# A two-layer decoder trunk on one core: weight splits around the norms move from GpSimd to VectorE in a new order, and u and the gates use three 256-column products

## The chip, the cores and the metric

The kernel runs on 1 core of one Trainium2 chip. The metric is the time of one execution in microseconds (us) of device time, lower is better.

## The reference

Two decoder layers over 256 tokens with 2048 features, in float32. Cut to what matters here:

```python
# layer 0: one input projection, its columns split into q, k, v, the forget gates, and u
proj = x @ w_in                       # 2048 -> 3*1024 + 8 + 1024
fox  = forgetting_attention(q, k, v, f_logit + b_f)     # 8 heads x 128
y    = s5_scan(u, ...)                                  # 64 groups x 16 channels, complex state of 64
ssm  = glu(gelu(y) @ w_glu)
mix  = concat(fox, ssm) @ w_out
# layer 1: sliding-window attention instead, 32 q heads / 4 kv heads x 64
# every layer:
x = LN(alpha*x + mix)
x = LN(alpha*x + (silu(gate) * val) @ w_down)   # gate, val: causal 3-wide conv of x @ w_up, d_ff 5504
```

## The kernel before

**Products in two parts.** Every weight comes as float32 in chunks of 128 x 1024 (512 KB) and is split into a high part `hi`, which ScalarE casts to the matmul type (line 110), and a rest `lo = raw - hi`, which VectorE subtracts (line 115). The activations `xT` are split in the same way: `xT[:, k, 0]` is the high part and `xT[:, k, 1]` the rest, for each of 16 blocks `k` of 128 features. A product is hi·hi + hi·rest + lo·hi; the last of the four is left out. There are two forms:

- `bmm` (line 412) has the weights stationary. It multiplies the 512 columns of `xT[:, k]` (high part and rest, 256 tokens each) by `hi`, into the two halves of a PSUM bank, and then the 256 high columns by `lo`, into the second half. `joined` (line 417) adds the halves: ScalarE copies the second half to SBUF, and VectorE adds the first.
- `amm` (line 421) has the activations stationary and streams 512 columns of weights, in three products into one bank.

**The stream.** `Stream` holds the list of all chunks in the order of use. SP loads them into 5 raw buffers. `done` frees the chunk just used, splits what there is room for (4 pairs of `hi` and `lo` at most are held) and then steps the side generators (`pump`), which record a little VectorE, ScalarE and TensorE work of the scan (`s5_gen`), the attention heads and so on between the weight chunks. So the order on every engine is the order in which the Python code runs; each engine works its queue strictly in that order, and waits where a semaphore of another engine is missing.

**The start (lines 1338 to 1385).** u is computed in 8 tiles of 128 columns, two chunks each, in two rounds of four tiles (`bmm`, 8 per chunk). After the second chunk of a tile, `joined` makes `ut`, the ScalarE queue sends `ut` to memory (line 1357), and after every second tile the GpSimd queue fetches it back in another layout (`load_u4`, line 1336). The chunk of the forget gates follows (16 `bmm`, then `joined` into `ft`, which `fox_gate` transposes at line 1232), then v (`a_run`). Beside all this VectorE prepares the scan: tables (`tab`), turned on TensorE at line 1040, and GpSimd multiplies phasors (lines 294 to 296).

**The boundaries.** There are three places where a layer norm stands between two big products (`boundary`): after the mixer of layer 0, after its FFN, and after the mixer of layer 1. The last 8 chunks before it (`tail`) and the first 8 after it (`head`) are each run twice, for token block `tb` 0 and 1, so that TensorE has work while the norm is computed. The first four chunks of the head are held in the usual pairs; the other four are split into free room of a later tensor ("places"). Lists of steps, one per chunk, say what is recorded between the products:

- `s` splits the next chunk; `s0` and `s1` interleave the split in quarters (line 127) with the statistics of block 0 or 1 (`ln_stats`);
- `n` and two digits: the norm of block tb, quarter q (`norm`, one VectorE instruction of 128x512 at line 228);
- `t`: TensorE turns that quarter (4 transposes, line 500), ScalarE scales it (line 504) and casts its high part (line 508);
- `l`: VectorE subtracts the rest of that quarter (line 213). An `amm` of the head on it needs both parts.

`PLAN_TAIL` runs beside the second pass of the tail, `PLAN_MID` between tail and head, and `PLAN_HEAD` beside the head: its first 8 entries stand behind head chunks 0 to 7 of block 0, the others behind those of block 1. `POOL_LO` sends the subtraction of the last head chunk (7) to GpSimd.

Of the kernel before, what the change touches and what calls it, by code (L numbers as in the profile page):

```python
# [21 lines left out]
P = 128  # L22
T = 256
D = 2048
KT = D // P
# [4 lines left out]
LCH = 4  # L30
# [15 lines left out]


PLAN_TAIL = "s0 n00 n01", "s n02", "s", "s", "t00", "t01 n03", "l00", "t02 l01"
PLAN_MID = "s1 l02"
PLAN_HEAD = ("s", "t03 n10 l03 n11", "", "s n12 n13 s", "", "t10", "t11 l10", "l11 t12",  # L50
             "t13 l12", "", "l13", "", "", "", "", "")
POOL_LO = {"t": (), "h": (7,)}

C_ID, C_TRI, C_CM, C_BM, C_M8, C_IF, C_N = 0, 128, 256, 384, 512, 520, 528

# [1 line left out]
class Stream:  # L57
# [31 lines left out]
    def split_next(self, steps=None, late=False):  # L89


        i = self.split
        size, dst = self.items[i][1:]
        r = self.raws.pop(i)[:, :size]
        eng = self.nc.vector
        if dst is None:
            hi = self.parts.tile([P, CH], F32R, tag="hi", name=f"hi{i}")
            lo = self.parts.tile([P, CH], F32R, tag="lo", name=f"lo{i}")
            self.held += 1
            o = hi[:, :size], lo[:, :size]  # L100
        elif dst[0] == "x":
            o = dst[1:]
            r = r.rearrange("p (a b) -> p a b", a=o[0].shape[1])
        else:
            o = [t_[:, :size] for t_ in self.places[dst[1]](dst[2])]
            self.busy.add(dst[1:3])
            if dst[3]:
                eng = self.nc.gpsimd
        hi, lo = o
        self.nc.scalar.copy(hi, r)  # L110
        self.outs[i] = o
        self.split += 1

        def rest():
            eng.tensor_tensor(lo, r, hi.bitcast(F32), op=ALU.subtract)  # L115
            self.out -= dst is None or dst[0] != "x"
            self.load()

        if late:
            return rest  # L120
        if steps is None:
            rest()
            return
        next(steps)
        m = size // 4
        for c in range(0, size, m):
            eng.tensor_tensor(lo[:, c:c + m], r[:, c:c + m], hi[:, c:c + m].bitcast(F32), op=ALU.subtract)  # L127
            next(steps, None)
            next(steps, None)
        for _ in steps:  # L130
            pass
        self.out -= 1
        self.load()
# [67 lines left out]
def trunk(ctx: ExitStack, tc: tile.TileContext, A, out):  # L201
    nc = tc.nc
    V, S, PE, G = nc.vector, nc.scalar, nc.tensor, nc.gpsimd
# [14 lines left out]
    def add(o, a, b):  # L218
        tt(o, a, b, ALU.add)
# [13 lines left out]
    def mm(o, l, r, start, stop):  # L233
        PE.matmul(o, lhsT=l, rhs=r, start=start, stop=stop)  # L234
# [84 lines left out]
    xT = mk(xtp, [P, KT, 2, T], F32R)  # L319
# [12 lines left out]

    def ext(place, c):

        return ("at", place, c - 4, c in POOL_LO[place[0]]) if c >= 4 else None

    for i0 in (0, 4):
        for h in range(2):
# [72 lines left out]
    def bmm(ps, hi, lo, k, first, last):  # L411


        mm(ps, hi, xT[:, k].rearrange("p a t -> p (a t)"), first, False)
        mm(ps[:, T:], lo, xT[:, k, 0, :], False, last)

    def joined(o, ps, view=lambda a: a):
        S.copy(o, view(ps[:, T:]))  # L418
        add(o, o, view(ps[:, :T]))

    def amm(o, hi, lo, src, k, tb, first, last):

# [64 lines left out]
    def boundary(li, tail, resid, after_tail, head):  # L487
# [3 lines left out]
        with tc.tile_pool(name="lnp", bufs=1) as lp:  # L491
# [50 lines left out]
            after_tail()  # L542
            do(PLAN_MID)
            part = []
            for c in range(8):
                part.append(st.get())
                head(part[c], 0, c)
                do(PLAN_HEAD[c])
            for c in range(8):
# [790 lines left out]
    for i0 in (0, 4):  # L1340
        ps = [bank(acc) for _ in range(4)]
        for c in range(2):
            for i in range(i0, i0 + 4):
                hi, lo = st.get()
                xs = 4 if i == 0 else 0
                for _ in range(xs):
                    st.get()
                o = ps[i - i0]
                for j in range(8):
                    bmm(o, hi[:, j * P:(j + 1) * P], lo[:, j * P:(j + 1) * P], 8 * c + j, c + j == 0, c == 1 and j == 7)  # L1350
                for _ in range(xs):
                    st.free()
                st.done()
                if c == 1:
                    ut = mk(s5w, [P, LCH, NCH], tag="ut", bufs=2)
                    joined(ut, o, lambda a: a.rearrange("p (n l) -> p l n", l=LCH))
                    S.dma_start(out=ud[P * i:P * i + P], in_=ut)
                    if i % 2 == 1:
                        load_u4(i // 2)
                    if i == 2:  # L1360
                        consts_round()
# [4 lines left out]
    ps = bank(acc)  # L1366
    hi, lo = st.get()
    for k in range(KT):
        bmm(ps, hi[:, 8 * k:8 * k + P], lo[:, 8 * k:8 * k + P], k, k == 0, k == KT - 1)
    st.done()  # L1370
    ft = mk(fp, [8, T])
    joined(ft, ps[0:8])
    gate = st.add(fox_gate(ft, fp))


# [10 lines left out]
    for h in range(H0):  # L1386
        qk = []
        for j in range(2):
            ps = bank(acc)
            b_tile(ps, 2)  # L1390
            t_ = mk(fp, [P, T], tag=f"qk{j}", bufs=2)
            if j == 0:
                c = 1.0 / math.sqrt(128.0)
# [9 lines left out]
    for cc, a, b in O0:  # L1403
# [12 lines left out]
        if b == 4:  # L1416
            for tb in range(2):
                o = stash[:, tb, cc * 512:(cc + 1) * 512]
# [10 lines left out]
    for ks in (range(0, 6), range(6, 8)):  # L1429
        for c in range(4):  # L1430
            hi, lo = part[c]
# [31 lines left out]
    last = [[bank(acc), bank(acc)] for _ in range(2)]  # L1463
# [131 lines left out]
```

## Time and profile before

| | us |
|---|---|
| median of 3 runs | 2136.7 (2136.3 to 2136.89) |
| the profiled execution | 2135.78 |
| its span | 2134.0 |
| TensorE matmul busy | 2089.1 (98%) |
| VectorE busy | 1464.5 (69%) |
| ScalarE busy | 1110.9 (52%) |
| GpSimd busy | 74.7 (3%) |

The profiled execution's own time is its span and 1.8 us around it; it lies 0.9 us under the median. Matmuls are pipelined, so their busy time is a sum of overlapping records; how fast TensorE works is read from the distance of their starts, and what it loses from the waits.

### The profile page before, as it was taken

How to read it: one execution, taken by the hardware profiler on the slowest of the kernel's cores; microseconds unless marked ns; L12 is line 12 of the kernel's file. 1: busy time of each engine (PE TensorE's matmuls, PEld its weight loads, DVE VectorE, ACT ScalarE, POOL GpSimd, SP SyncE). 2: the span in 40 equal slices, each digit the busy share in tenths (PEclk: the TensorE clock that was granted, in tenths of full speed). 3: DMA queues.
4: the chain of work that ended last, by engine and by line, in shares of the span. 5: the costliest groups of instructions: out<-in, count | busy, mean ns of one | idle time of the engine just before them, and what ended most of it. 6: DMA issues, size and time to landing. Idle time of an engine off the chain costs nothing.

```text
span 2134.0 us, 29675 instructions
## 1 busy us (share of the span) xinstructions
PE 2089.1 (98%) x11084; PEld 1759.7 (82%) x11084; DVE 1464.5 (69%) x2325; ACT 1110.9 (52%) x1766; POOL 74.7 (3%) x143
## 2 busy tenths in 40 slices
PE   8899999999999999999999999999999999999997
PEld 7688878788888888888887878778888888888886
DVE  6888866868777777744446867678777777754445
ACT  4355455566555555533336566475555555543332
POOL 3600000000000000000001000000000000000000
PEclk9999999999999999999999999999999999999999
DMA  7454455656656666566565634647666666666564
GB/s 264 151 154 135 129 193 173 202 177 213 191 188 189 190 193 189 180 192 191 183 192 165 191 119 129 197 152 229 192 190 188 189 194 190 188 188 190 185 188 158
DMA packets 111456, 388.84 MB, mean 182 GB/s; under 512 B 13072, under 2 KB 15120, under 8 KB 111056
## 3 DMA queue, kind: packets, MB, share of 16 engines
q1 hardware_dynamic: 104112, 371.37, 55.5%
q10 hardware_dynamic: 5712, 10.20, 1.9%
q0 software_dynamic: 1488, 5.38, 0.8%
q8 instruction: 87, 1.43, 0.3%
q14 instruction: 57, 0.47, 0.1%
HBM read 383.75 MB, written 3.15 MB: 181 GB/s over the span
## 4 chain that ended last, share of the span: by engine, by line
PE 90%; DVE 6%; ACT 2%; DMA 1%; issue 1%; POOL 0%; SPq 0%; ACTq 0%; DVEq 0%; POOLq 0%
PE bank L234 88%; DVE lo L115 2%; DVE t L213 1%; DVE t L231 1%; DVE z L213 1%; ACT hi L110 1%; DMA raw<-wu 1%; DVE t L228 1%; DMA t<-x 0%; PE bank L1040 0%; PE bank L500 0%; DVE t L115 0%; PE bank L829 0%; ACT x L504 0%; DVE t L127 0%
## 5 line engine op out<-in xcount | busy, mean ns | idle before, releaser
L115 DVE TENSOR_TENSOR lo<-raw,hi 128x1024 fp32r<-128x1024 f32 (+1 forms) x674 | 819.0, 1219 | 526.8 <-ACT hi L110 525.5
L234 PE MATMUL bank<-t,hi 128*128 128x512 f32 x3152 | 1101.0, 395 | 7.5 <-DVE t L115 7.5
L110 ACT CAST hi<-raw 128x1024 fp32r<-128x1024 f32 x677 | 705.1, 1047 | 651.3 <-PE bank L234 566.0
L234 PE MATMUL bank<-t,lo 128*128 128x256 f32 x3152 | 877.5, 278 | 1.8 <-DVE lo L115 1.8
L234 PE MATMUL bank<-hi,t 128*128 128x512 f32 x2248 | 723.0, 398 | 1.3 <-DVE ut L213 1.3
L234 PEld LDWEIGHTS bank<-t,hi 128*128 128x128 f32 x3152 | 592.7, 188 | 145.5 <-DVE t L115 7.5
L234 PEld LDWEIGHTS bank<-t,lo 128*128 128x128 f32 x3152 | 593.8, 188 | 3.2 <-DVE lo L115 3.0
L234 PEld LDWEIGHTS bank<-hi,t 128*128 128x128 f32 x2248 | 424.3, 189 | 104.3 <-issue 3.8
L234 PE MATMUL bank<-lo,t 128*128 128x512 f32 x1124 | 445.0, 396 | 2.2 <-DVE lo L115 2.2
L234 PEld LDWEIGHTS bank<-lo,t 128*128 128x128 f32 x1124 | 212.5, 189 | 51.8 <-DVE lo L115 3.7
L231 DVE SCALAR_TENSOR_TENSOR y<-h,t,y 128x255 f32<-128x255 f32 (+1 forms) x328 | 136.4, 478 | 0.5 <-ACT y L634 0.5
L418 ACT COPY h<-bank 128x256 f32<-128x256 f32 x164 | 60.2, 373 | 87.5 <-PE bank L234 85.0
L234 PE MATMUL bank<-t,t 128*128 128x512 f32 (+3 forms) x422 | 89.6, 357 | 9.9 <-DVE t L115 7.7
L634 ACT ACTIVATE y<-h,t 128x256 f32<-128x256 f32 x164 | 89.9, 597 | 15.2 <-DVE h L213 15.1
L234 PEld LDWEIGHTS bank<-t,t 128*128 128x128 f32 (+1 forms) x422 | 63.0, 177 | 23.3 <-DVE t L115 8.6
L213 DVE TENSOR_TENSOR h<-h,bank 128x256 f32<-128x256 f32 x164 | 66.9, 421 | 21.2 <-ACT h L418 21.2
L813 ACT ACTIVATE p<-bank,sm 128x128 f32<-128x128 f32 (+1 forms) x64 | 26.1, 419 | 45.2 <-DVE sm L213 45.2
L504 ACT ACTIVATE x<-bank,t 128x128 f32<-128x128 f32 x96 | 36.1, 456 | 19.6 <-PE bank L500 18.3
L643 ACT ACTIVATE y<-y 128x256 f32<-128x256 f32 x86 | 35.5, 413 | 20.2 <-DVE y L231 20.2
L237 ACT CAST t<-y 128x256 fp32r<-128x256 f32 x86 | 34.3, 400 | 5.4 <-DVE y L213 5.3
L213 DVE TENSOR_TENSOR t<-y,t 128x256 fp32r<-128x256 f32 x86 | 35.8, 419 | 0.9 <-ACT t L237 0.9
L213 DVE TENSOR_TENSOR y<-y,y 128x256 f32<-128x256 f32 x86 | 35.9, 419 | 0.3
(174 smaller groups left out, 976.3 us busy)
## 6 DMA issues: line engine op xcount, KB each, us to landing
raw<-wup SPq DMA_DIRECT2D x328, 512.0 KB, 3.7
raw<-wdn SPq DMA_DIRECT2D x168, 512.0 KB, 4.2
raw<-wo SPq DMA_DIRECT2D x64, 512.0 KB, 3.7
raw<-wi SPq DMA_DIRECT2D x40, 512.0 KB, 3.9
raw<-wqk SPq DMA_DIRECT2D x32, 512.0 KB, 3.6
raw<-wu SPq DMA_DIRECT2D x16, 512.0 KB, 5.2
raw<-wv SPq DMA_DIRECT2D x16, 512.0 KB, 3.7
raw<-wg SPq DMA_DIRECT2D x16, 512.0 KB, 4.0
```

The lines of the kernel that those rows point to most:

```text
L110: self.nc.scalar.copy(hi, r)
L115: eng.tensor_tensor(lo, r, hi.bitcast(F32), op=ALU.subtract)
L213: V.tensor_tensor(o, a, b, op=op)
L228: V.tensor_scalar(o, a, s1, s2, op0=op0, op1=op1)
L231: V.scalar_tensor_tensor(o, a, s, b, op0=op0, op1=op1)
L234: PE.matmul(o, lhsT=l, rhs=r, start=start, stop=stop)
L237: S.copy(hi, src)
L418: S.copy(o, view(ps[:, T:]))
L504: S.activation(x32[:, j], pt[:, j * P:(j + 1) * P], AF.Identity, bias=lnT[:, li, 1, k:k + 1], scale=lnT[:, li, 0, k:k + 1])
L634: S.activation(y[e], ps[e][:, :T], AF.Identity, bias=cw[:, n, 3:4], scale=cw[:, n, 2:3])
L643: S.activation(y[0], y[0], AF.Silu)
L813: S.activation(pp[:, e], vv[:, e], AF.Exp, bias=sm[:, 0, qb, e:e + 1], scale=1.0, accum_out=sm[:, 2, qb, e:e + 1])
```

## The change

Three things. (1) `POOL_LO` goes: no head chunk is split on GpSimd, so VectorE subtracts all four "places". (2) The steps in the middle and beside the head are reordered; the tail's are as before. (3) u and the gates use `bmm3`, three products of 256 columns into one half of the bank, so that their sum is complete in PSUM and a ScalarE copy takes the place of `joined`. `joined` stays for the other users, without the view.

```diff
-PLAN_MID = "s1 l02"
-PLAN_HEAD = ("s", "t03 n10 l03 n11", "", "s n12 n13 s", "", "t10", "t11 l10", "l11 t12",
-             "t13 l12", "", "l13", "", "", "", "", "")
-POOL_LO = {"t": (), "h": (7,)}
+PLAN_MID = "l02 s1"
+PLAN_HEAD = ("n10 s", "t03 l03 s", "s n11", "", "", "t10 n12", "l10", "t11 n13",
+             "l11 t12", "t13 l12", "l13", "", "", "", "", "")
@@ split_next
             o = [t_[:, :size] for t_ in self.places[dst[1]](dst[2])]
             self.busy.add(dst[1:3])
-            if dst[3]:
-                eng = self.nc.gpsimd
@@ ext
-        return ("at", place, c - 4, c in POOL_LO[place[0]]) if c >= 4 else None
+        return ("at", place, c - 4) if c >= 4 else None
@@
-    def joined(o, ps, view=lambda a: a):
-        S.copy(o, view(ps[:, T:]))
-        add(o, o, view(ps[:, :T]))
+    def bmm3(ps, hi, lo, k, first, last):
+
+        mm(ps, hi, xT[:, k, 0, :], first, False)
+        mm(ps, hi, xT[:, k, 1, :], False, False)
+        mm(ps, lo, xT[:, k, 0, :], False, last)
+
+    def joined(o, ps):
+        S.copy(o, ps[:, T:])
+        add(o, o, ps[:, :T])
@@ u
-                o = ps[i - i0]
+                o = ps[i - i0][:, :T]
                 for j in range(8):
-                    bmm(o, hi[:, j * P:(j + 1) * P], lo[:, j * P:(j + 1) * P], 8 * c + j, c + j == 0, c == 1 and j == 7)
+                    bmm3(o, hi[:, j * P:(j + 1) * P], lo[:, j * P:(j + 1) * P], 8 * c + j, c + j == 0, c == 1 and j == 7)
...
-                    joined(ut, o, lambda a: a.rearrange("p (n l) -> p l n", l=LCH))
+                    S.copy(ut, o.rearrange("p (n l) -> p l n", l=LCH))
                     S.dma_start(out=ud[P * i:P * i + P], in_=ut)
@@ gates
-        bmm(ps, hi[:, 8 * k:8 * k + P], lo[:, 8 * k:8 * k + P], k, k == 0, k == KT - 1)
+        bmm3(ps[:, :T], hi[:, 8 * k:8 * k + P], lo[:, 8 * k:8 * k + P], k, k == 0, k == KT - 1)
     st.done()
     ft = mk(fp, [8, T])
-    joined(ft, ps[0:8])
+    S.copy(ft, ps[0:8, :T])
```

Of the instructions, 144 `bmm` become 144 groups of three (8 tiles x 16, and 16 for the gates); 9 VectorE additions go; 3 subtractions of 128x1024 move from GpSimd to VectorE. In the rows below the changed kernel's lines are 3 lower up to `amm` and 3 higher behind it (its line 112 is the subtraction of 115, its 1360 the transfer of 1357).

**ScalarE's queue behind the first u tile** (`ut` is the tile of u, `t_164` the memory that it is sent to, `hi` the cast of the next weight chunk; in brackets the semaphores that a row waits for). Before:

```order
L110 CAST hi_318<-raw_142 128x1024 [waits DMAHW2_49,DVE_49,PE_49]
L418 COPY ut_329<-bank_167 128x256 [waits PE_49]
L1357 DMA t_164<-ut_329 128x256 [waits DMAHW7_49,DVE_49]
L110 CAST hi_349<-raw_148 128x1024 [waits DMAHW3_49,Activation_49]
L418 COPY ut_361<-bank_168 128x256 [waits PE_49]
L1357 DMA t_164<-ut_361 128x256 [waits DVE_49]
L110 CAST hi_386<-raw_241 128x1024 [waits DMAHW4_49,Activation_49]
```

And in the changed kernel:

```order
L107 CAST hi_358<-raw_142 128x1024 [waits DMAHW2_49,DVE_49,PE_49]
L1359 COPY ut_369<-bank_167 128x256 [waits PE_49]
L1360 DMA t_164<-ut_369 128x256 [waits Activation_49]
L107 CAST hi_396<-raw_148 128x1024 [waits DMAHW3_49,DVE_49]
L1359 COPY ut_408<-bank_168 128x256 [waits PE_49]
L1360 DMA t_164<-ut_408 128x256 [waits Activation_49]
L107 CAST hi_440<-raw_257 128x1024 [waits DMAHW4_49,DVE_49]
```

The places in the queue are the same. The transfer of `ut`, and with it the cast behind it, no longer waits for VectorE's addition, but for ScalarE's own copy.

**VectorE's queue at the first boundary**, from the end of `s1` on (`t_4070` and `t_4205` are the places of head chunks 4 to 7; `t_3238` and `t_3373` hold x, so that a 128x512 TENSOR_SCALAR is an `n`; `t_77<-x_...` is an `l`). Before:

```order
L127 TENSOR_TENSOR t_4070<-raw_3878,t_4070 128x256
L231 SCALAR_TENSOR_TENSOR t_114<-t_114 128x1 x3
L213 TENSOR_TENSOR t_77<-x_357_4052,t_77 128x4x128
L115 TENSOR_TENSOR t_4070<-raw_3956,t_4070 128x1024
L228 TENSOR_SCALAR t_3238<-t_3238,t_114 128x512
L213 TENSOR_TENSOR t_77<-x_363_4115,t_77 128x4x128
L228 TENSOR_SCALAR t_3238<-t_3238,t_114 128x512
L115 TENSOR_TENSOR t_4070<-raw_3970,t_4070 128x1024
L228 TENSOR_SCALAR t_3238<-t_3238,t_114 128x512 x2
L213 TENSOR_TENSOR t_77<-x_365_4163,t_77 128x4x128
```

And in the changed kernel:

```order
L124 TENSOR_TENSOR t_4205<-raw_4013,t_4205 128x256
L228 SCALAR_TENSOR_TENSOR t_114<-t_114 128x1 x3
L225 TENSOR_SCALAR t_3373<-t_3373,t_114 128x512
L112 TENSOR_TENSOR t_4205<-raw_4091,t_4205 128x1024
L210 TENSOR_TENSOR t_77<-x_363_4251,t_77 128x4x128
L112 TENSOR_TENSOR t_4205<-raw_4105,t_4205 128x1024
L112 TENSOR_TENSOR t_4205<-raw_4118,t_4205 128x1024
L225 TENSOR_SCALAR t_3373<-t_3373,t_114 128x512 x2
L210 TENSOR_TENSOR t_77<-x_365_4296,t_77 128x4x128
L225 TENSOR_SCALAR t_3373<-t_3373,t_114 128x512
```

`l02` has gone to before `s1` (it stands above this piece, directly behind the last residual); n10 goes first, chunks 5, 6 and 7 are subtracted with only `l03` between them, and n11 to n13 follow. On TensorE, t10 stays behind head chunk 5 of block 0; t11 goes from behind chunk 6 to behind chunk 7, t12 from behind chunk 7 to behind chunk 0 of block 1, and t13 from there to behind chunk 1.

**TensorE, the first products of u** (`t_77` is xT). Before:

```order
L234 MATMUL bank_167<-t_77,hi_118 128x512
L234 MATMUL bank_167<-t_77,lo_119 128x256
L234 MATMUL bank_167<-t_77,hi_118 128x512
L234 MATMUL bank_167<-t_77,lo_119 128x256
L234 MATMUL bank_167<-t_77,hi_118 128x512
```

And in the changed kernel:

```order
L231 MATMUL bank_167<-t_77,hi_118 128x256 x2
L231 MATMUL bank_167<-t_77,lo_119 128x256
L231 MATMUL bank_167<-t_77,hi_118 128x256 x2
L231 MATMUL bank_167<-t_77,lo_119 128x256
L231 MATMUL bank_167<-t_77,hi_118 128x256 x2
```

The columns are the same, 768 for a block of features; what was one product of 512 columns is two of 256, each with a weight load of its own.

## Rows read from the trace of the kernel before

**Rows 1.** The profile's fourth part: the chain of work that ended last, by engine.

```profile
PE 90%; DVE 6%; ACT 2%; DMA 1%; issue 1%; POOL 0%; SPq 0%; ACTq 0%; DVEq 0%; POOLq 0%
```

**Rows 2.** What TensorE waited for longest over the whole span: us in total, times, longest.

```profile
PE bank L234 <- DVE t L115: 15.2, 4, 7.5
```

**Rows 3.** Stretches of the span: length, then busy us (instructions) of PE, PEld, DVE, ACT, POOL, then the granted TensorE clock as a share of 2.4 GHz, DMA share, GB/s.

```profile
76.00:87.00 11.00, 8.10 (x38) 6.55 (x38) 10.75 (x23) 3.37 (x6) 10.35 (x20) 0.69 0.62 195
424.00:432.00 8.00, 6.98 (x30) 5.72 (x31) 3.17 (x5) 4.59 (x12) 0.00 (x0) 0.79 0.42 133
1151.00:1159.00 8.00, 5.98 (x23) 4.93 (x24) 3.88 (x6) 3.93 (x11) 0.54 (x1) 0.79 0.46 143
1405.00:1413.00 8.00, 5.43 (x30) 4.26 (x29) 6.13 (x7) 3.68 (x10) 2.93 (x1) 1.00 0.66 221
```

**Rows 4.** TensorE in order of time, the start of the kernel: start us, us, then the instruction, and in brackets the idle time before it and what ended it. The first two stand in the u tiles; the gates end at 62.83, where v begins.

```profile
39.32 0.39 PE L234 MATMUL bank<-t,lo 128*128 128x256 f32 x1 [0.69 <-DVE lo L115]
...
43.25 0.39 PE L234 MATMUL bank<-t,lo 128*128 128x256 f32 x1 [0.76 <-DVE lo L115]
...
62.83 0.41 PE L234 MATMUL bank<-hi,t 128*128 128x512 f32 x1
...
76.17 0.29 PE L1232 MATMUL bank<-t,t 8*128 8x8 f32 x2 [3.67 <-DVE t L213]
78.70 1.94 PE L1040 MATMUL bank<-t,t 128*128 128x128 f32 x8 [2.24 <-POOL t L295]
80.29 0.78 PE L234 MATMUL bank<-hi,t 128*128 128x512 f32 x1
...
85.11 1.04 PE L1040 MATMUL bank<-t,t 128*128 128x128 f32 x8
```

**Rows 5.** ScalarE: one cast in order of time; and from the answer on the tile `ut`: VectorE's additions (ns, least, median, most; first and last start), and what ScalarE waited for them (us, times).

```profile
61.64 1.05 ACT L110 CAST hi<-raw 128x1024 fp32r<-128x1024 f32 x1 [4.45 <-DVE ut L213]
```

```profile
L213 DVE TENSOR_TENSOR ut<-ut,bank x8: 407/413/415, 27.1 to 70.9; 128x256 f32<-128x256 f32 x8
...
  ACT hi L110: 27.6, 7
```

**Rows 6.** VectorE in order of time in the same stretch; the last row is the end of the table that line 1040 turns.

```profile
62.72 1.23 DVE L115 TENSOR_TENSOR lo<-raw,hi 128x1024 fp32r<-128x1024 f32 x1 [1.54 <-ACT hi L110]
...
68.18 1.48 DVE L115 TENSOR_TENSOR lo<-raw,hi 128x1024 fp32r<-128x1024 f32 x1 [1.54 <-ACT hi L110]
...
72.77 1.22 DVE L115 TENSOR_TENSOR lo<-raw,hi 128x1024 fp32r<-128x1024 f32 x1 [1.48 <-ACT hi L110]
...
77.18 2.05 DVE L213 TENSOR_TENSOR t<-z,z 64x512 f32<-64x512 f32 x3
```

**Rows 7.** TensorE in order of time: a pair of products in a u tile; then the scores of the sliding-window attention, which multiply 256 columns by a high part twice and by a rest once, with a load before each. Last, the profile's group of weight loads of the high parts (busy us, mean ns | idle before).

```profile
30.12 0.40 PE L234 MATMUL bank<-t,hi 128*128 128x512 f32 x1
30.35 0.28 PE L234 MATMUL bank<-t,lo 128*128 128x256 f32 x1
30.46 0.40 PE L234 MATMUL bank<-t,hi 128*128 128x512 f32 x1
...
1201.01 0.51 PE L234 MATMUL bank<-t,qT 128*128 128x256 f32 x3
1201.36 0.28 PE L234 MATMUL bank<-t,t 128*128 128x256 f32 x1
```

```profile
L234 PEld LDWEIGHTS bank<-t,hi 128*128 128x128 f32 x3152 | 592.7, 188 | 145.5 <-DVE t L115 7.5
```

**Rows 8.** TensorE in order of time at the boundaries: the first from head chunk 4 on, then the long wait of the third.

```profile
418.01 0.63 PE L234 MATMUL bank<-t,t 128*128 128x512 f32 x2
419.18 2.60 PE L234 MATMUL bank<-t,t 128*128 128x512 f32 x10 [0.53 <-DVE t L213]
...
421.97 0.48 PE L234 MATMUL bank<-t,t 128*128 128x512 f32 x1
425.02 1.81 PE L234 MATMUL bank<-t,t 128*128 128x512 f32 x5 [2.57 <-DVE t L115]
...
1409.67 1.43 PE L234 MATMUL bank<-t,t 128*128 128x512 f32 x5 [2.57 <-DVE t L115]
```

**Rows 9.** The other engines at the first boundary, in order of time: VectorE, GpSimd, ScalarE (of its rows, the cast of t02 and the two pairs of casts of head chunks 4 to 7).

```profile
415.61 0.42 DVE L127 TENSOR_TENSOR t<-raw,t 128x256 fp32r<-128x256 f32 x1 [1.01 <-ACT t L110]
...
417.92 0.60 DVE L231 SCALAR_TENSOR_TENSOR t<-t 128x1 f32<-128x1 f32 x3
418.44 0.68 DVE L213 TENSOR_TENSOR t<-x,t 128x512 fp32r<-128x512 f32 x1
419.04 1.22 DVE L115 TENSOR_TENSOR t<-raw,t 128x1024 fp32r<-128x1024 f32 x1
420.17 0.54 DVE L228 TENSOR_SCALAR t<-t,t 128x512 f32<-128x512 f32 x1
...
421.23 2.60 DVE L228 TENSOR_SCALAR t<-t,t 128x512 f32<-128x512 f32 x1
```

```profile
420.61 2.93 POOL L115 TENSOR_TENSOR t<-raw,t 128x1024 fp32r<-128x1024 f32 x1 [136.06 <-ACT t L110]
```

```profile
414.01 0.62 ACT L508 CAST t<-x 128x512 fp32r<-128x512 f32 x1
...
418.49 1.99 ACT L110 CAST t<-raw 128x1024 fp32r<-128x1024 f32 x2
```

## The prediction, made before the changed kernel was run

> **What bounds the kernel now.** I read the chain of waits first. TensorE is 90% of the chain that ends last [rows 1]: a change pays where it takes away a wait of TensorE, or shortens its products, and nowhere else. So next comes the list of what TensorE waited for. Its largest entry is VectorE's subtractions, 15.2 us in four waits; one of 7.5 is the first product's wait at the start, which the change leaves alone, and the other three make 7.7 [rows 2]. They are one long wait of about 2.57 us in each of the three boundaries [rows 8]. The other waits are smaller and stand in the first 80 us, where TensorE in order of time shows them [rows 4]. Last I read the granted clock in stretches: behind the waits at 72 to 80 us, and behind the long wait of the first and the second boundary, TensorE ran at 1.2 GHz for a while. Behind that of the third it did not [rows 3].
>
> **The long wait at a boundary: why it is there.** At the first boundary GpSimd's subtraction runs from 420.61 for 2.93 us, to 423.54. VectorE starts n11, a norm of 128x512, at 421.23; it takes 2.60 us, to 423.83, where the same instruction took 0.54 us just before [rows 9]. So VectorE's norm stood still until GpSimd was done. Behind it in VectorE's queue stands the subtraction of head chunk 6, for which TensorE waits from 421.97 on: its next product starts at 425.02 [rows 8]. 512 columns are otherwise 0.23 us apart [rows 7], so the wait costs 3.05 - 0.23 = 2.82 us, three times 8.5 us. To this comes the clock: (1 - 0.79) x 8 us = 1.7 us at the first and at the second boundary, nothing at the third [rows 3], 3.4 us. With no subtraction on GpSimd the cause is gone.
>
> **What takes its place.** I walk through the first boundary with the durations of rows 9.
> - `l02` first: ScalarE has t02's cast at 414.63, and VectorE idled until 415.61 for the cast of chunk 4. `l02` (0.68) fits in that hole, so `s1` is not later than before. This takes away the short wait at chunk 4, whose third product had to wait for `l02` until 419.12, worth some 0.5 us.
> - `s1` ends at 418.5. Then come n10 (0.45 from start to start), chunk 5 (1.14), `l03` (0.60), chunk 6 (1.14; cast by 419.5) and chunk 7 (1.14; cast by 420.5). They end at 419.0, 420.1, 420.7, 421.9 and 423.0.
> - TensorE runs chunk 4 from 418.0 to 419.4. Its second product of chunk 5, at 419.6, needs the subtraction of chunk 5: a **new wait** of 0.5 us. Chunk 5 then ends near 421.4, t10 at 421.8. Chunk 6 needs its subtraction at 422.0 (there at 421.9), chunk 7 at 423.4 (there at 423.0). t11 at 424.6 needs n11 (423.5). So the block runs through, and t12 and t13, now between the products of block 1, are needed only two chunks later.
>
> The 0.5 us lost at chunk 5 and the 0.5 us won at chunk 4 cancel. The 3.7 us of subtractions that GpSimd did are new on VectorE, in the shadow of TensorE's products as long as the last slack, 0.1 and 0.4 us, holds; that is the thinnest place of this prediction. GpSimd has no other work at this boundary. **Boundaries: 8.5 + 3.4 = 11.9 us.**
>
> **The three narrow products.** 144 times, a product of 512 and one of 256 columns become three of 256, and one weight load is added. A pair takes 0.34 us in the u tiles. Three products of 256 columns with a load before each, twice by the same high part and once by a rest, take 0.35 us in the scores of layer 1 [rows 7]. So columns count, not products, and the edit costs TensorE nothing; the 0.01 us, if it is more than rounding, makes 1.4 us in 144, which I keep as the upper bound. The far bound is that the loads set the pace, at their mean of 188 ns [rows 7]; that is the third rival.
>
> The Trainium skill's page "TensorE: Matmul & The Clock Gate" says in its Part 3, "The mechanism", that a load overlaps running products only when it goes to another row group, and gives 128 columns of weights about 107 ns under "LDWEIGHTS (loading the stationary operand)". By that rule the 144 added loads would lie bare, an estimate of 15.4 us more. The trace speaks against it: four loads and products in a row at 0.117 us each leave no room for a bare 107 ns.
>
> **The start.** Here the gain is not on TensorE but in the queue of ScalarE. Before, the transfer of `ut` waits for VectorE's addition, and the next weight's cast stands behind that transfer. Casts lost 27.6 us so, in seven waits, one of them 4.45 us [rows 5]. VectorE then waits about 1.5 us for that cast before it can subtract [rows 6], and TensorE for the subtraction. With the sum complete in PSUM, copy, transfer and cast follow each other on ScalarE without VectorE. What TensorE lost:
> - in the u tiles 0.69 and 0.76 us idle [rows 4], with some 0.2 us of restart each 1.9 us;
> - from 62.83 to 80.29, 17.46 us for 36 products of 0.23 (8.3), two tiny transposes (0.3) and eight transposes (1.0): 9.6 us of work, so 7.9 us of waits, with 3.67 for the gates' addition among them [rows 4];
> - the next chunk, 12 products from 80.29 to 85.11, 4.82 instead of 2.8 us at 1.2 GHz: 2.0 us [rows 3, 4]. The clock fell behind the idle time and should stay up without it.
>
> Sum 11.8 us, if VectorE keeps up. The tightest point is the first half of the table that line 1040 turns. It was ready near 78.6 [rows 6]. TensorE will want it at 62.83 - 1.9 + 8.6 = 69.5, so VectorE has to be 9.1 us earlier. It loses 1.5 us of idle time and 0.41 us for the addition at each u tile [rows 5, 6]. The last three gaps and four additions make 6.2 us; five tiles before offer 9.5 us more, of which three are needed. At most four pairs are held, so it can't be much further ahead; an estimate with that limit puts the half table at 66. **Start: 11.8 us.**
>
> **Sum.** 11.9 + 11.8 = 23.7 us. Against the profiled execution, 2135.8 - 23.7 = 2112.1; the median of the runs lies 0.9 above it, so **2113.0 us**.
>
> **The rivals.**
> 1. *VectorE's scan sets the pace of the start.* The scan's work on VectorE and GpSimd is the same as before; if it, not the addition, held the weights back, TensorE finds new waits at line 1040 and later, and the start gains nothing. For it: VectorE was busy 10.75 of 11 us from 76 to 87 [rows 3]. Against it: the three idle gaps ended by casts [rows 6]. Time 2113.0 + 11.8 = 2124.8.
> 2. *The thin slack at the boundaries breaks.* If chunk 6 or 7 comes one subtraction later than walked, each boundary loses 1.22 us again: 2113.0 + 3.7 = 2116.7. For it: slack of 0.1 to 0.4 us. Against it: before, the same instructions ran back to back in just these times [rows 9].
> 3. *Weight loads set the pace of the narrow products, and the kernel is slower.* Place: u and the gates. If each of the three takes a load's 188 ns, a group takes 0.564 instead of 0.34 us, 144 times 32.3 us: 2113.0 + 32.3 = 2145.3. It decides the sign from 0.168 us per product on (23.7 / 144 + 0.34 = 0.505, by three). The scores' 0.117 speaks against it; but those runs are four long, not 24.
>
> **How the numbers follow.** Forecast 0.70, rival 1 0.12, rival 2 0.10, rival 3 0.05, anything else 0.03. About 0.2%, 4.3 us, is what a measurement here tells from no change; the forecast and rivals 1 and 2 all lie below 2132.4. So faster 0.92, same 0.03, slower 0.05. The range: 1.5 us less if no wait comes up at chunk 5, and 1.4 more of the start's clock loss ((1 - 0.69) x 11 = 3.4 instead of 2.0 [rows 3]), with the spread of runs 2108 as the low end. At the high end rival 2 is in, with the 1.4 us of narrow products, and a start that gains half: 2122. Rival 1 in full and rival 3 stay out.
>
> **What would show it.** Right: no subtraction of line 115 on GpSimd; no norm of 128x512 over 0.6 us; no wait of TensorE over 1 us in the boundaries and one near 0.5 us at chunk 5; the clock at 1.00 through 70 to 90 us and behind all three boundaries; pairs of products of 256 columns 0.117 us apart in the u tiles; casts that follow the copy of `ut` at once; line 1040 reached near 69 to 70 us. Wrong: the gates' transposes or line 1040 still waited for, or spacings over 0.12 us in the u tiles.

## The result, and the profile after

The changed kernel takes 2111.9 us (median of 4 runs, 2109.2 to 2115.9), the kernel before 2136.5 on the same chip; the ratio is 0.9889, 95% interval 0.987 to 0.9907. Run again later beside other kernels it took 2109.3 against 2135.3, ratio 0.9882 (0.9867 to 0.9897). The profiled execution took 2109.19, its span 2107.4. In the changed kernel's rows line 112 is the subtraction of a weight's rest, 107 the cast, 225 the norm, 210 `add` and `sub`, 231 the products, 1043 the table and 503 the turn of a quarter.

The chain of waits, as in [rows 1], and under it the start of the list of what TensorE waited for, as in [rows 2] (us in total, times, longest):

```profile
PE 94%; DVE 4%; ACT 1%; issue 1%; DMA 0%; SPq 0%; DVEq 0%; ACTq 0%
```

```profile
PE bank L231 <- ACT t L107: 5.9, 1, 5.9
PE bank L231 <- DVE t L112: 1.7, 4, 0.8
PE bank L231 <- ACT czn L1051: 1.3, 2, 0.7
PE bank L231 <- DVE lo L112: 1.1, 3, 0.4
...
PE bank L1192 <- ACT u L1179: 1.0, 1, 1.0
```

At the boundaries TensorE's waits for subtractions fall from 7.7 us to 0.9, which is the 1.7 without the 0.8 at the start. The start's long wait is not gone: the 7.5 us have become 5.9 for ScalarE's cast, since the first narrow product needs only the high part of xT, and 0.8 for the subtraction behind it. The gates' transposes and the table, 3.7 and 2.2 us before [rows 4], are gone from the list.

Stretches as in [rows 3] (the three boundaries, then the start; the granted clock is the third number from the end):

```profile
404.00:412.00 8.00, 7.56 (x39) 5.96 (x38) 5.97 (x8) 5.59 (x13) 0.00 (x0) 1.00 0.79 257
1127.00:1135.00 8.00, 7.75 (x38) 5.98 (x38) 6.52 (x9) 5.17 (x11) 0.00 (x0) 1.00 0.74 240
1379.00:1387.00 8.00, 7.74 (x38) 6.07 (x37) 6.81 (x11) 5.63 (x12) 0.00 (x0) 1.00 0.76 231
76.00:87.00 11.00, 10.51 (x78) 8.87 (x77) 9.60 (x29) 3.25 (x5) 9.96 (x28) 1.00 0.50 144
```

TensorE at the start, in order of time, as in [rows 4, 7]; the last product of the gates' chunk is at 61.43:

```profile
14.10 0.40 PE L231 MATMUL bank<-t,hi 128*128 128x256 f32 x2
14.34 0.28 PE L231 MATMUL bank<-t,lo 128*128 128x256 f32 x1
14.46 0.40 PE L231 MATMUL bank<-t,hi 128*128 128x256 f32 x2
...
61.56 0.39 PE L231 MATMUL bank<-hi,t 128*128 128x512 f32 x1
...
66.81 0.39 PE L231 MATMUL bank<-hi,t 128*128 128x512 f32 x1
67.13 0.28 PE L1235 MATMUL bank<-t,t 8*128 8x8 f32 x2
67.35 1.09 PE L1043 MATMUL bank<-t,t 128*128 128x128 f32 x8
68.20 0.48 PE L231 MATMUL bank<-hi,t 128*128 128x512 f32 x1
```

From v's first product to the table nothing waits: 6.64 us from 61.56 to 68.20, where it was 17.46 [rows 4]. Three narrow products take 0.36 us (14.10 to 14.46). On ScalarE the answer on the tile `ut`, which showed 27.6 us of waiting casts [rows 5], now has

```profile
  ACT hi L107: 0.5, 1
```

The first boundary, VectorE and then TensorE, as in [rows 8, 9] (403.35 is n10, 405.55 the subtractions of chunks 6 and 7, 407.82 n11 and n12):

```profile
403.35 0.55 DVE L225 TENSOR_SCALAR t<-t,t 128x512 f32<-128x512 f32 x1
403.81 1.22 DVE L112 TENSOR_TENSOR t<-raw,t 128x1024 fp32r<-128x1024 f32 x1
404.94 0.69 DVE L210 TENSOR_TENSOR t<-x,t 128x512 fp32r<-128x512 f32 x1
405.55 2.35 DVE L112 TENSOR_TENSOR t<-raw,t 128x1024 fp32r<-128x1024 f32 x2
407.82 1.00 DVE L225 TENSOR_SCALAR t<-t,t 128x512 f32<-128x512 f32 x2
```

```profile
402.85 1.80 PE L231 MATMUL bank<-t,t 128*128 128x512 f32 x7
405.08 1.44 PE L231 MATMUL bank<-t,t 128*128 128x512 f32 x5 [0.44 <-DVE t L112]
406.35 0.60 PE L503 MATMUL bank<-t,t 128*128 128x128 f32 x4
406.71 3.03 PE L231 MATMUL bank<-t,t 128*128 128x512 f32 x12
```

No norm is held up, and the only wait is at chunk 5's second product: its start is 0.83 us behind the first one's, 0.6 more than the usual 0.23 (0.40 and 0.41 more at the other two).

**Where the 26.8 us went.** The same product is compared in both traces: the changed kernel is 1.27 us ahead at v's first product (62.83 against 61.56), 12.1 at the first product behind the table (80.29, 68.20), 14.06 a chunk later. Until 367 us another 1.1 us come up, 0.5 of it at a wait for `u` (line 1192), which is no part of the change: the kernel before waits 1.6 us there, the changed kernel 1.0, and in its second profile 2.1. The boundaries add 4.5, 4.4 and 2.8. At the end it is 26.8 ahead (spans: 2134.0 - 2107.4 = 26.6).

### The profile page after: what moved, and what is told of

Same layout as the page of the kernel before. It is cut to its first block, busy times and chain, and to the rows that moved or that the text cites. A ratio compares the mean times of both kernels' runs of the same rounds, so it can differ in the third digit from the quotient of the medians.

```text
span 2107.4 us, 29935 instructions
## 1 busy us (share of the span) xinstructions
PE 2081.8 (99%) x11228; PEld 1762.4 (84%) x11228; DVE 1460.5 (69%) x2319; ACT 1112.4 (53%) x1766; POOL 70.0 (3%) x140
## 4 chain that ended last, share of the span: by engine, by line
PE 94%; DVE 4%; ACT 1%; issue 1%; DMA 0%; SPq 0%; DVEq 0%; ACTq 0%
PE bank L231 92%; DVE lo L112 1%; DVE z L210 1%; DVE t L228 1%; DVE t L210 0%; PE bank L503 0%; DMA raw<-wu 0%; PE bank L832 0%; PE bank L1043 0%; ACT hi L107 0%; ACT x L507 0%; DVE t L124 0%; DVE t L112 0%; PE bank L791 0%; PE bank L835 0%
## 5 line engine op out<-in xcount | busy, mean ns | idle before, releaser
L231 PE MATMUL bank<-t,hi 128*128 128x512 f32 (+1 forms) x3296 | 1101.5, 385 | 6.7 <-ACT t L107 5.9
L231 PEld LDWEIGHTS bank<-t,hi 128*128 128x128 f32 x3296 | 610.7, 188 | 137.9 <-ACT t L107 5.9
L637 ACT ACTIVATE y<-h,t 128x256 f32<-128x256 f32 x164 | 89.9, 598 | 15.9 <-DVE h L210 15.7
L507 ACT ACTIVATE x<-bank,t 128x128 f32<-128x128 f32 x96 | 36.1, 457 | 10.7 <-PE bank L503 9.3
```

The source lines that it names most:

```text
L507: S.activation(x32[:, j], pt[:, j * P:(j + 1) * P], AF.Identity, bias=lnT[:, li, 1, k:k + 1], scale=lnT[:, li, 0, k:k + 1])
L637: S.activation(y[e], ps[e][:, :T], AF.Identity, bias=cw[:, n, 3:4], scale=cw[:, n, 2:3])
```

## The experiments

**1. The two parts alone.** The kernel before with the narrow products only (e1), and with the new order and VectorE's subtractions only (e2).

```diff
 e1, in u and the gates, against the kernel before:
-                    bmm(o, hi[:, j * P:(j + 1) * P], lo[:, j * P:(j + 1) * P], 8 * c + j, c + j == 0, c == 1 and j == 7)
+                    bmm3(o, hi[:, j * P:(j + 1) * P], lo[:, j * P:(j + 1) * P], 8 * c + j, c + j == 0, c == 1 and j == 7)
-                    joined(ut, o, lambda a: a.rearrange("p (n l) -> p l n", l=LCH))
+                    S.copy(ut, o.rearrange("p (n l) -> p l n", l=LCH))
...
 e2, against the kernel before:
-PLAN_MID = "s1 l02"
+PLAN_MID = "l02 s1"
-POOL_LO = {"t": (), "h": (7,)}
...
```

> The kernel before, with the narrow products and the ScalarE copy for u and the gates alone; GpSimd's subtraction and the order at the boundaries as before. Theory (two independent parts): the start is 14.1 us earlier from the first chunk of v on, as in the trace of the changed kernel, and everything behind it too, so about 2122 (2136.5 - 14.1), 2120 to 2125; at the three boundaries TensorE waits 2.57 us again, with n11 near 2.6 us, and the clock falls to 1.2 GHz behind two of them. Rival (the parts need each other, since a late start moves what the boundary finds ready): the waits at the boundaries have another length, and the time is over 3 us from 2122. Rival (the sum's 11.8 us for the start): 2124.7.

> The kernel before, with the new order of steps and VectorE in GpSimd's place alone; u and the gates in wide products with VectorE's addition. Theory: the boundaries give 11.9 us as summed (4.5, 4.5 and 2.8), so 2124.6, 2123 to 2126.5; the start shows the old waits (3.67 and 2.24 us at the gates' transposes and line 1040's table) and the old fall of the clock. Rival (the clock behind a boundary depends on what came before and not on the wait): drops of the clock stay at one boundary or more, 1.7 us each, 2126 to 2128.

Narrow products alone: 2121.5 against 2136.5, ratio 0.9935 (0.9918 to 0.9952). The start is as in the changed kernel, 15.0 us ahead behind the table's chunk, and the boundary waits are there again, 2.56, 2.71 and 2.56 us (TensorE at the first; clock 0.83, 0.83 and 1.00 in the 10 us around the three boundaries):

```profile
406.32 0.48 PE L234 MATMUL bank<-t,t 128*128 128x512 f32 x1
409.35 1.94 PE L234 MATMUL bank<-t,t 128*128 128x512 f32 x5 [2.56 <-DVE t L115]
```

At the second boundary the expectation for n11 missed: what is held there is `l03`, just ahead of n11 in VectorE's queue, with 2.88 us instead of 0.68, and n11 takes 0.54. TensorE loses as much.

Boundaries alone: 2122.6, ratio 0.994 (0.9924 to 0.9957), two us better than the sum said. By stages the boundaries gave 4.5, 4.4 and 2.9, 11.7 in all, as forecast; the other 2 us lie outside them, 1.1 at the start, where this execution's clock came back sooner, and 1.0 between 85 and 367 us. These same differences of single executions stand in both kernels' gains, so 15.7 and 13.8 us add to more than 26.8. By the traces the parts are independent and the rivals fall: the start's gain is not 11.8, the waits with GpSimd cost what they did, and without it no boundary has a fall of the clock. The medians alone would not settle it: 15.0 and 13.9 us make 28.9, against 24.6 and 26.0 for both parts, and the interval of each is some 3.5 us either way.

**2. Order or engine at the boundary.** The changed kernel with the old lists of steps, all on VectorE; and with its own lists, chunk 7 on GpSimd:

```diff
 e3, against the changed kernel:
-PLAN_MID = "l02 s1"
-PLAN_HEAD = ("n10 s", "t03 l03 s", "s n11", "", "", "t10 n12", "l10", "t11 n13",
+PLAN_MID = "s1 l02"
+PLAN_HEAD = ("s", "t03 n10 l03 n11", "", "s n12 n13 s", "", "t10", "t11 l10", "l11 t12",
...
 e4, against the changed kernel:
+POOL_LO = {"t": (), "h": (7,)}
+            if dst[3]:
+                eng = self.nc.gpsimd
...
```

> The changed kernel with the old order of steps at the boundaries, but VectorE subtracts chunk 7 (no GpSimd). Theory (the wait was GpSimd holding up n11): n11 takes 0.54 us; chunk 6's subtraction ends about 1.2 us after n11's start, 0.7 to 0.8 us late for TensorE, chunk 7's some 0.3 us late behind n12 and n13, and the third product of chunk 4 waits for l02 0.5 us again. So the wait of 2.57 us is gone without the new order, the clock stays at 2.4 GHz, and the boundary costs about 1.5 us, against 0.4 to 0.6 in the changed kernel: 2112 to 2116 (3 us above the changed kernel). Rival (the order was the cause): a wait of 2.5 us at chunk 6 and the clock's fall stay, 2120 to 2124.

> The changed kernel with its new order of steps, but GpSimd subtracts chunk 7 again. Theory (GpSimd holds up a norm on VectorE, and it costs what waits behind that norm): GpSimd starts when chunk 7 is cast, 405.3 to 405.9 in the changed kernel's times, and takes 2.9 us; n11, at 406.7, is held until near 408.5; chunk 6's subtraction now stands ahead of n11 and is not held. TensorE wants chunk 7's subtraction at 408.3, so it waits 0 to 0.5 us there, no wait over 1 us and no fall of the clock: 0 to 1.5 us above the changed kernel, 2109 to 2115. So the new order alone would take the long wait away. Rival (a subtraction on GpSimd brings the wait in any order): a wait of over 2 us in each boundary, 2119 to 2124.

The old order without GpSimd: 2112.35 in one run. VectorE (n11, then chunk 6's subtraction) and TensorE:

```profile
406.21 0.54 DVE L225 TENSOR_SCALAR t<-t,t 128x512 f32<-128x512 f32 x1
406.67 1.22 DVE L112 TENSOR_TENSOR t<-raw,t 128x1024 fp32r<-128x1024 f32 x1
```

```profile
404.16 2.61 PE L231 MATMUL bank<-t,t 128*128 128x512 f32 x10 [0.51 <-DVE t L210]
...
407.94 1.44 PE L231 MATMUL bank<-t,t 128*128 128x512 f32 x5 [0.49 <-DVE t L112]
```

n11 takes its 0.54 us, the long wait is gone, and two short ones stay. The theory holds.

The new order with GpSimd: 2119.85 in one run. Here **the theory's expectation failed**: it let n11 be held and chunk 6's subtraction go free. VectorE (chunk 6's subtraction, n11 and n12), GpSimd and TensorE:

```profile
407.02 3.41 DVE L115 TENSOR_TENSOR t<-raw,t 128x1024 fp32r<-128x1024 f32 x1
410.35 0.99 DVE L228 TENSOR_SCALAR t<-t,t 128x512 f32<-128x512 f32 x2
```

```profile
406.89 2.46 POOL L115 TENSOR_TENSOR t<-raw,t 128x1024 fp32r<-128x1024 f32 x1 [136.28 <-ACT t L110]
```

```profile
408.19 0.48 PE L234 MATMUL bank<-t,t 128*128 128x512 f32 x1
410.49 2.37 PE L234 MATMUL bank<-t,t 128*128 128x512 f32 x9 [1.81 <-DVE t L115]
```

GpSimd began 0.13 us before VectorE's subtraction of chunk 6 and held this one: 3.41 us instead of 1.22, ending 1.08 us behind GpSimd's end. TensorE waited 1.81 us in each boundary. So it is not the norm alone that GpSimd's subtraction holds up, but a subtraction as well, and neither of the two orders is saved from the wait. An order in which VectorE has nothing due at that time was not tried.

Gains of the boundaries against the kernel before, from the same products in each trace: old order without GpSimd 3.4 + 3.4 + 1.8 = 8.6 us; new order with GpSimd 2.3 + 0.8 - 0.8 = 2.3; both 11.6. Three quarters belong to GpSimd, the order gives the last 3.

The Trainium skill's page "SBUF — State Buffer", "SBUF: two separate sides", says that VectorE and GpSimd share one port pair as an exclusive lock: the instruction that starts first has it to its end, and the other stands still (of VectorE's instructions those in a two-port mode, and those with two SBUF inputs where GpSimd's reads SBUF). That one stands still behind the other agrees with n11 [rows 9], though no row says in which mode a norm runs, and with chunk 6's subtraction, which ended 1.08 us behind GpSimd's in all three boundaries of experiment 2. Who comes first the rows don't settle: in the kernel before, GpSimd's record begins 0.02, 0.08 and 0.02 us ahead of `l03`'s, and yet `l03` took its usual 0.69 us, and GpSimd 2.93 to 2.99 us instead of the 2.46 here. At the second boundary of e1 it begins 0.07 us ahead, and there `l03` was held and GpSimd took 2.40. Either way TensorE waited 2.6 to 2.7 us.

**3. Narrow products or ScalarE's queue.** Two half steps: wide products and VectorE's addition as before, but the transfer of `ut` issued one chunk later, behind the next cast; and narrow products, but VectorE copies the finished sum.

```diff
 e5, against the boundaries alone:
                 st.done()
+                while after:
+                    after.pop()()
...
-                    S.dma_start(out=ud[P * i:P * i + P], in_=ut)
-                    if i % 2 == 1:
-                        load_u4(i // 2)
+                    def send(i=i, ut=ut):
+                        S.dma_start(out=ud[P * i:P * i + P], in_=ut)
+                        if i % 2 == 1:
+                            load_u4(i // 2)
+                    after.append(send)
 e6, against the changed kernel (and the same for ft):
-                    S.copy(ut, o.rearrange("p (n l) -> p l n", l=LCH))
+                    V.tensor_copy(ut, o.rearrange("p (n l) -> p l n", l=LCH))
```

> The new order at the boundaries as in the changed kernel; u and the gates in wide products with VectorE's addition as before, but the transfer of each u tile (and the fetch back behind every second one) is issued one weight chunk later, behind the next cast in ScalarE's queue. It separates the shape of the products from ScalarE's queue. Theory (the casts stood behind a transfer that waited for VectorE's addition): casts no longer wait 2.5 to 4.5 us, and the start gains nearly as much as with narrow products: 10 to 13 us of the 14, because VectorE still makes eight additions of 0.41 us, while TensorE saves 1.5 us on the wide products; 2110 to 2116. Rival (the gain came from the narrow products, a sum that is complete in PSUM earlier, or from one addition less on VectorE): nothing from the later transfer, 2123 to 2126 as for the boundaries alone. A middle value near 2118 would say that the fetch back, now later, holds up the scan.

> The changed kernel with one thing undone: VectorE, not ScalarE, copies the finished sum of u and of the gates from PSUM. Products stay narrow; the transfer of ut waits for VectorE again, with the next cast behind it. Theory (ScalarE's queue): the casts wait 2.5 to 4 us again in the u tiles, and of the start's 14 us some 9 to 12 go back: 2121 to 2125, with waits of TensorE at the gates' transposes and the clock's fall between 70 and 90 us. Rival (the narrow products, or VectorE's work on an addition, were the gain): a copy takes VectorE as long as the addition did or less, and the time stays within 2 us of the changed kernel, 2110 to 2114.

Wide with the late transfer: 2111.7, ratio 0.9894 (0.9877 to 0.991), as fast as the changed kernel. In its answer on `ut` no cast waits any more, and TensorE has no wait in u behind the first product. ScalarE still idles for `ut`, but at its copies (line 415), with the next chunk's cast done:

```profile
  ACT ut L415: 9.5, 4
```

Narrow with VectorE's copies: 2123.2, 0.9949 (0.9934 to 0.9964), as the boundaries alone. In the latter the answer on `ut`, and TensorE at the gates and the table:

```profile
  ACT hi L107: 28.5, 6
```

```profile
76.20 0.38 PE L1235 MATMUL bank<-t,t 8*128 8x8 f32 x2 [3.72 <-DVE t L1375]
78.73 1.94 PE L1043 MATMUL bank<-t,t 128*128 128x128 f32 x8 [2.15 <-POOL t L292]
```

This is the start of before [rows 4, 5], with narrow products. So the product's shape gives nothing; what pays is that the next chunk's cast no longer stands behind a transfer that waits for VectorE. Behind the table's chunk the late transfer is 10.8 us ahead of the boundaries alone, the changed kernel 13.0. The rest is rival 1 in small; TensorE with the late transfer:

```profile
65.41 0.28 PE L1229 MATMUL bank<-t,t 8*128 8x8 f32 x2 [1.09 <-DVE t L210]
67.94 1.27 PE L1037 MATMUL bank<-t,t 128*128 128x128 f32 x6 [2.25 <-DVE t L210]
```

It is 2.9 us ahead of the changed kernel at the end of u (1.6 of it in the wide products; the other 1.3 stand in the first two chunks, where e1, with the narrow products, is 1.0 ahead as well), but VectorE has the table only at 67.8, so it stands and then loses some at 1.2 GHz (clock 0.91 from 64 to 84 us).

**4. VectorE's time alone.** The changed kernel, with the nine additions as work that nobody waits for, behind the transfer:

```diff
                     S.dma_start(out=ud[P * i:P * i + P], in_=ut)
+                    add(ps[i - i0][:, T:].rearrange("p (n l) -> p l n", l=LCH), ut, o.rearrange("p (n l) -> p l n", l=LCH))
...
+    add(ps[0:8, T:], ft, ps[0:8, :T])
```

> The changed kernel with VectorE's nine additions put back as work that nobody needs: behind the transfer of each u tile (and behind the copy of the gates) VectorE adds the copied tile to the sum in PSUM once more, into the unused half of the bank. ScalarE's copy, transfer and cast are as in the changed kernel. It asks what VectorE's time at the start is worth without ScalarE's wait (rival 1 of the prediction). In the changed kernel TensorE reaches the table at line 1043 at 67.35, and its half is ready at about 66.7, 0.65 us before. Theory (VectorE is next in line there): some 8 x 0.33 us more work puts the table 2 to 2.7 us later, TensorE waits 1.3 to 2 us at line 1043 or at the gates' transposes, and the clock may fall behind that for another 0.5 to 1.6 us: 2113 to 2117, 1.5 to 4 us slower. Rival (VectorE has idle time ahead of the table that takes the additions in): no wait, 2110 to 2114.

2109.7, ratio 0.9881 (0.9867 to 0.9896): not to be told from the changed kernel, 2109.3 in the same comparison. TensorE at the table:

```profile
67.85 1.06 PE L1043 MATMUL bank<-t,t 128*128 128x128 f32 x8 [0.88 <-POOL t L292]
```

The half table is VectorE's and was ready at 67.71, 0.14 us before the row's start, as with the late transfer, where the row names VectorE. Here it names GpSimd, whose instruction ended in between. The wait came up, but with 0.88 us instead of 1.3 to 2, and no fall of the clock: the table came 1.0 us later (1.4 us, counted from v's first product), so between half and two thirds of the 2.7 us of additions went into VectorE's idle time. The time is the rival's, the wait a smaller one than the theory's.

**5. The price of a narrow product**, magnified: the three products in all other places of the wide form.

```diff
     def bmm(ps, hi, lo, k, first, last):
-        mm(ps, hi, xT[:, k].rearrange("p a t -> p (a t)"), first, False)
+        mm(ps[:, :T], hi, xT[:, k, 0, :], first, False)
+        mm(ps[:, T:], hi, xT[:, k, 1, :], False, False)
         mm(ps[:, T:], lo, xT[:, k, 0, :], False, last)
```

> The changed kernel with three narrow products in all the other places that use the wide form too: 3008 more groups (144 before). It magnifies the price of the narrow form. In the u tiles a group takes 0.3595 us in place of 0.349, 10.5 ns more. Theory (that price is the same everywhere): 3008 x 10.5 ns = 31 us slower than the changed kernel, 2143, 2138 to 2148. Rival (columns count, not products: the 0.117 us spacing of the attention scores): no change, 2112. Rival (a weight load of 188 ns sets the pace): 3008 x (0.564 - 0.349) = 647 us slower, 2759.

2146.6, ratio to the kernel before 1.0057 (1.0042 to 1.0072), and 34.7 us above the changed kernel's first median: 34.7 / 3008 = 11.5 ns a group (12.4 above its second median). The price is real, and small; the weight loads' 188 ns [rows 7] set no pace.

**6. The wait that is left.** The split of chunk 5 ahead of n10; then also that of chunk 6 ahead of `l03`, with the changed kernel run beside it:

```diff
 e8, against the changed kernel:
-PLAN_HEAD = ("n10 s", "t03 l03 s", "s n11", "", "", "t10 n12", "l10", "t11 n13",
+PLAN_HEAD = ("s n10", "t03 l03 s", "s n11", "", "", "t10 n12", "l10", "t11 n13",
 e10, against the changed kernel:
-PLAN_HEAD = ("n10 s", "t03 l03 s", "s n11", "", "", "t10 n12", "l10", "t11 n13",
+PLAN_HEAD = ("s n10", "t03 s l03", "s n11", "", "", "t10 n12", "l10", "t11 n13",
```

> The changed kernel with one step exchanged: at the first step of the head the split of chunk 5 goes ahead of n10. It goes for the wait that is left at each boundary, 0.59, 0.40 and 0.41 us at chunk 5's second product. Theory: chunk 5's subtraction starts 0.46 us earlier, so the three waits shrink to 0.13 us or nothing, and n10 is still ready long before t10: 1.2 us less in all, spacings under 0.4 us in the trace; in the time it can't be told from the changed kernel (2106 to 2114). Rival (chunk 5's cast on ScalarE, not VectorE, comes last): the waits stay above 0.3 us.

> The changed kernel with two steps of the head exchanged: the split of chunk 5 ahead of n10 (as tried alone before) and the split of chunk 6 ahead of l03. In the run with the first exchange alone the wait at chunk 5 was gone and chunk 6's second product waited 0.24 us (spacing 0.563 against 0.320 behind transposes). Theory: chunk 6's subtraction now ends 0.6 us earlier and that wait goes too; l03 ends at about the time of chunk 6's third product, and chunk 7's subtraction is 0.1 us late at worst. The three boundaries lose nothing over 0.15 us each: 1.4 to 1.8 us less than the changed kernel, about 2110.4, at the edge of what five rounds can tell. Rival (l03 now comes last): a new wait of 0.2 to 0.6 us at chunk 6's third product, and no gain.

> The changed kernel itself once more, on the same chip as the two others, for a comparison with them: 2112, 2109 to 2116, as in its first runs.

The first exchange (2109.7 in one run) takes chunk 5's wait away, and 0.24, 0.18 and 0.20 us come up at chunk 6 of the three boundaries. With both, chunks 4 and 5 run through, and 6 and 7 behind t10 (TensorE, 12 products each):

```profile
404.76 3.13 PE L231 MATMUL bank<-t,t 128*128 128x512 f32 x12
407.73 0.60 PE L503 MATMUL bank<-t,t 128*128 128x128 f32 x4
408.09 3.16 PE L231 MATMUL bank<-t,t 128*128 128x512 f32 x12
```

Each boundary is 0.42 to 0.46 us shorter than in the changed kernel's second profile, 1.3 us in three, just under the 1.4 to 1.8 expected. The time, 2108.7 (ratio 0.9877, 0.986 to 0.9893) against 2109.3, can't show so little: that this version is faster stands in the boundaries of its trace alone.

## Why the prediction was right

It said 2113.0, 23.7 us less; the median came to 2111.9, 24.6 less, within the 2108 to 2122. The mechanisms were right. That the first median comes within 1.1 us of the forecast is partly luck: the start alone gave 2.3 us more than its sum, with the narrow products' price taken off, and the later comparison has 26.0 us. Step by step:

- **Boundaries, 11.9 us: 11.6.** The mechanism was right as to GpSimd, as experiment 2 shows. The new wait at chunk 5, forecast at 0.5 us, was 0.6, 0.4 and 0.4, and the wait at chunk 4 went. The clock's 3.4 us came back. The thin slack of 0.1 and 0.4 us held, and rival 2 didn't come. Too narrow was the statement that a *norm* is held up: a subtraction is held in the same way.
- **Narrow products, 0: a loss of 1.0 to 1.9 us.** The upper bound of 1.4 should have been the value, or a little more: the 0.01 us was no rounding, and 144 times the 11.5 ns of experiment 5 is 1.7. Eight groups take 2.88 us, against 2.83 for eight pairs in the execution before and 2.77 in that of the boundaries alone; 18 chunks make 1.0 and 1.9. Rival 3 fell: at 0.120 us a product, 0.188 us of load can't lie bare. The estimate of 15.4 us took half of what the Trainium skill's page "TensorE: Matmul & The Clock Gate", Part 3 "The mechanism", says: besides another row group, the section names the background weight buffer as a place for which a load is pulled ahead of running products. The 1.7 us speak against the first half alone; no run shows where the loads go.
- **The start, 11.8: 14.06, with one term mis-sized.** The u tiles gave 1.3 (1.9 forecast, the narrow products' price taken off). The clock gave 2.0 as forecast, but that is a figure of one execution: behind the same waits at the gates and the table, the chunk that took 4.82 us took 3.6 with the boundaries alone and 3.7 with VectorE's copies, against 2.8 without a fall. The stretch from 62.83 to 80.29 gave not 7.9 but 10.8. The step that failed is "36 products of 0.23 (8.3)": there are 24 (two chunks of v), 5.5 us, as 61.56 to 66.81 in the rows of after shows. With the right count the loss comes to 17.46 - 5.5 - 0.3 - 1.0 = 10.7 us, 0.7 of it the eight transposes at the lower clock. The same slip put line 1040 at 69.5; TensorE was there at 67.35.
- **What was read off the list of waits.** The first product's wait was to be left alone; it was split in two, and the third product starts 0.4 us earlier (7.65 instead of 8.05). Nor did all the other waits stand in the first 80 us: the 1.6 us for `u` at line 1189 come at 300 us.
- **VectorE, rival 1.** The half table was ready at about 66.7 (forecast 66), so the rival stayed out, by 0.65 us and not by the 3.5 that the forecast had. Experiments 3 and 4 show that it is next: with the additions left in, the table comes at 67.8 and 67.7.

In the two profiled executions the gain is 26.8 us by the products, 3.1 above the sum: 2.3 from the start and 1.1 from between 85 and 367 us, where single executions differ, less 0.3 at the boundaries. The first median lies nearer to the sum: the profiled execution was the fastest of its four.

## What to carry to other kernels

An engine that casts, copies and issues transfers is one queue: before counting its busy time, look at what each transfer in it waits for, since one that waits for another engine stops all that stands behind it (here casts, for 27.6 us). A subtraction given to GpSimd was not free for VectorE: it added 2.1 to 2.2 us to the instruction that VectorE started behind it. Look at who waits for that one. Where a product's form changes, take the difference between two rows as a price until a magnified run says otherwise.

## What was not expected of the hardware

- **GpSimd and VectorE, both with SBUF operands:** what VectorE started behind GpSimd's subtraction stood still until that was done: 2.60 us for a norm of 0.54, 3.41 for a subtraction of 1.22, 2.88 for an `l` of 0.68 (e1). Where both began within 0.1 us, it was now the one that was held and now the other. A fill on GpSimd did not do this. In the changed kernel the fill runs from 1120.42 to 1123.95, and VectorE's `l` within it takes its usual 0.69:

```profile
1120.42 3.53 POOL L761 MEMSET t<- 128x4096 f32 x1 [850.05 <-DVE t L210]
```

```profile
1123.02 0.69 DVE L210 TENSOR_TENSOR t<-x,t 128x512 fp32r<-128x512 f32 x1 [0.28 <-ACT t L511]
```

- **The clock behind equal waits.** 2.57 us brought 1.2 GHz at the first two boundaries and not at the third [rows 3], and so did 2.56, 2.71 and 2.56 us with the narrow products alone. With the 1.81 us of experiment 2 it was the last two and not the first:

```profile
405.00:415.00 10.00, 7.71 (x37) 5.73 (x36) 7.41 (x8) 5.53 (x12) 2.46 (x1) 1.00 0.67 211
1131.00:1141.00 10.00, 7.94 (x31) 5.86 (x30) 7.05 (x8) 3.55 (x8) 2.52 (x1) 0.83 0.69 209
1387.00:1397.00 10.00, 7.92 (x31) 5.86 (x30) 6.94 (x7) 3.98 (x9) 2.46 (x1) 0.83 0.62 208
```

  What decides is open; 1.7 us hang on it each time.
